# First phase of a two-layer hybrid decoder trunk: the state-space parameter work spread over sixteen steps, three modulation steps summed on VectorE

## The chip, the cores and the metric

The kernel runs on one core of one Trainium2 chip. The metric is the time of one execution on the device in microseconds (us), as the median of several runs. A second view is one profiled execution, whose trace lists each instruction of each engine with its start and its length. The engines are PE (TensorE, the matrix engine), DVE (VectorE), ACT (ScalarE), POOL (GpSimd) and SP (SyncE, which here only issues loads). Each engine takes its instructions in one fixed order; an instruction that waits holds all that stand behind it on its engine.

## The reference

The reference is a decoder trunk of two layers on 256 tokens of width 2048. What matters here is the head of layer 0:

```python
mod = jax.nn.silu(c) @ w_ada[layer] + b_ada[layer]
sh1, sc1, g1, sh2, sc2, g2 = jnp.split(mod, 6, axis=-1)
h = x * (1.0 + sc1[:, None, :]) + sh1[:, None, :]
...
proj = h @ w_in
...
dt = jnp.exp(log_dt)[:, None]
mag = jnp.exp(lam_re * dt)
lb_re = mag * jnp.cos(lam_im * dt)
lb_im = mag * jnp.sin(lam_im * dt)
...
_, _, x_re, x_im = lax.associative_scan(_complex_affine_combine, (a_re, a_im, bu_re, bu_im), axis=1)
```

A conditioning vector `c` gives a shift and a scale for each of the 2048 input channels (a matrix-vector product). The modulated input goes through the input projection `w_in`; one part of it, `u`, feeds a diagonal complex recurrence (S5) whose parameters (step size, decay, rotation, input and output matrices) are worked out from small weights that don't depend on the tokens. The other part feeds attention. Later come the output projection, layer norms, a SwiGLU block, and layer 1 with windowed attention. All is float32 in and out; a projection is made of three matrix products of split operands (a high part and a low part of each).

## The kernel before

**The first phase** is a loop over 16 steps `k`, one for each block of 128 input channels. All weights of the program come through a ring of 9 slots (`RING`), each a piece of 128x1024 float32 or less, in one fixed order on SP's queue; a piece is loaded when the piece nine places before it has been released. Each step takes six pieces. Four pieces (512 KB each, tensor `ada_s`) hold the columns of `w_ada` for the shift and the scale of the step's 128 channels; two pieces (384 KB each, `w_s`) hold 12 tiles of the input projection. A step does this:

- L660: 16 matmuls (the trace records each as two) multiply the four `ada_s` pieces with the conditioning vector into a PSUM bank `ab`; ACT copies the bank (L664), two small matmuls (L666) fold it to two columns, and DVE adds the bias (L668, tile `mod`): the step's shift and scale.
- DVE modulates the step's input (L670, tile `x`), ACT rounds it to the high part (L671, tile `hp`), and DVE subtracts for the low part (L672).
- `split` (L271 on ACT, L272 on DVE) makes the high part `wh` and the low part `wl` of each `w_s` piece, in three buffers (`NSPLIT`). The piece is released when both are done.
- 36 matmuls (L613, L614, L615) add the step to the banks of 12 output tiles. In this text they are the step's projection matmuls.

The bank `ab` is one, so the L660 matmuls of a step start only after the L668 of the step before.

**The recurrence's parameters** (`s5_params`, a generator) run beside the loop. Each call of `adv` takes the generator to its next `yield`; before, each step calls it twice (`EK[3]`). In the order of the code: step size and decay (128x32 operations, 12 to 20 in a chain), sine and cosine of the angle on ACT, four complex powers and three products as separate 128x32 operations (`cmul`, six operations each), then four quarters of a 128x2048 cosine and sine table (L470, L473, L474 on DVE, three activations L475 to L477 on ACT for each quarter), then the output matrices times the four powers (24 operations of 128x512, L485 to L491), then four quarters of the input matrices: six operations of 128x512 on DVE (L502 to L508), four activations on ACT (L511, tile `ebd`), 16 transposes on PE with four copies on ACT (L516, L517), 16 small matmuls `kc` (L524) and a copy on DVE (L528). Behind the loop the generator is run to its end. The table is first used after the phase, by the recurrence itself (L759, L760).

**What sets the order.** The code gives an order; a scheduler then reorders on each engine by its own estimate of the times, except that instructions marked with `front` are put ahead. So the place of the parameter work on an engine is neither that of the code nor fixed by hand. The loads keep the order of the code.

**After the loop** PE multiplies the forget-gate weights (L690), ACT copies the banks out (L703, L705) and re-lays `u` for the recurrence (L730), and the stream of weight pieces goes on: projection tiles (`w_ab`) and further pieces of `w_ada`. Most of those are multiplied and summed on DVE by one `tensor_tensor_reduce` for each piece (L544), with a row of the conditioning vector (`crow`), which steps 1 to 4 of the loop spread over the partitions.

Of the kernel before, what the change touches and what calls it, by code (L numbers as in the profile page):

```python
# [13 lines left out]
AF = mybir.ActivationFunctionType  # L14
# [16 lines left out]
FIRST = 3  # L31
EK = (1, 4, 1, 2)
HEAD = (10, 10, 10)
# [242 lines left out]
def build(tc, I, out):  # L276
# [3 lines left out]
    with ExitStack() as es:  # L280
# [98 lines left out]
        def s5_params():  # L379
# [5 lines left out]
            def tt(o, a, b, op):  # L385
                V.tensor_tensor(o, a, b, op)
# [22 lines left out]
            tt(th, lim, dt, ALU.mult)  # L409
            rho, sn, co, u0 = reg[8:12]  # L410
            V.tensor_scalar(t1, th, 1.0 / (2 * math.pi), MAGIC, op0=ALU.mult, op1=ALU.add)
# [12 lines left out]
            yield  # L424
            lr = [None, reg[12], reg[8], reg[10], reg[15]]
            li = [None, reg[13], reg[9], reg[14], reg[5]]
            tt(lr[1], mag, co, ALU.mult)
# [19 lines left out]

            def cmul(orr, oi, ar_, ai, br, bi):
                tt(t0, ar_, br, ALU.mult)
                tt(t1, ai, bi, ALU.mult)  # L450
                tt(t2, ar_, bi, ALU.mult)
                tt(t3, ai, br, ALU.mult)
                tt(orr, t0, t1, ALU.subtract)
                tt(oi, t2, t3, ALU.add)

            for k in (2, 3, 4):
                cmul(lr[k], li[k], lr[k - 1], li[k - 1], lr[1], li[1])
            for k in (1, 2, 3):
                cmul(wvr[:, 3 - k, :], wvi[:, 3 - k, :], lr[k], li[k], qr, qi)
            yield  # L460
# [6 lines left out]

            for qd in range(4):
                ca, sa = cosT[:, 512 * qd:512 * qd + 512], sinT[:, 512 * qd:512 * qd + 512]
                V.tensor_tensor(w1.rearrange("p (a j) -> p a j", j=64),  # L470
                                u0[:, 8 * qd:8 * qd + 8].rearrange("p (a o) -> p a o", o=1).to_broadcast([128, 8, 64]),
                                jrow.rearrange("p (o j) -> p o j", o=1).to_broadcast([128, 8, 64]), ALU.mult)
                V.tensor_scalar(w2, w1, MAGIC, -MAGIC, op0=ALU.add, op1=ALU.add)  # L473
                V.tensor_tensor(w1, w1, w2, ALU.subtract)  # L474
                A.activation(sa, w1, AF.Sin, scale=TWO_PI_LO)  # L475
                A.activation(ca, w1, AF.Abs)
                A.activation(ca, ca, AF.Sin, scale=-TWO_PI_LO, bias=hpi)  # L477
                yield

            V.tensor_scalar(gci[:, 0:512], gci[:, 0:512], -1.0, None, op0=ALU.mult)  # L480
            cr0, ci0 = a3(gcr[:, 0:512]), a3(gci[:, 0:512])
            for k in range(1, 5):
                orr = a3(g4[0]) if k == 4 else gcv[0][:, k]
                oi = a3(g4[1]) if k == 4 else gcv[1][:, k]
                V.tensor_tensor(orr, cr0, bc(lr[k]), ALU.mult)  # L485
                V.tensor_tensor(a3(w1), ci0, bc(li[k]), ALU.mult)
                V.tensor_tensor(orr, orr, a3(w1), ALU.add)
                yield
                V.tensor_tensor(oi, ci0, bc(lr[k]), ALU.mult)
                V.tensor_tensor(a3(w2), cr0, bc(li[k]), ALU.mult)  # L490
                V.tensor_tensor(oi, oi, a3(w2), ALU.subtract)  # L491
                yield

            eb = ebd.rearrange("p (c x g h) -> p c x g h", c=2, g=2, h=16)
            ebf = ebd.rearrange("p (c a m) -> p c a m", c=2, a=8)
            for qd in range(4):
# [30 lines left out]
                yield  # L527
                V.tensor_copy(kc[:, H], b[:, 0:128])  # L528


# [108 lines left out]
        ada0 = [scr[:, 256 * i:256 * i + 256] for i in range(2)]  # L639
        mod0 = c.small(32, "mod0")  # L640
        m0v = mod0.rearrange("p (t v) -> p t v", v=2)
        bad0 = c.small(32, "bad0")
# [11 lines left out]
        for k in range(KT):  # L654
            early.get(k, lambda: None)()
            for q in range(4):
                t = c.ptiles[6 * k + q]
                for j in range(4):
                    kk = 4 * q + j
                    PE.matmul(abank[32 * j:32 * j + 32, 0:256], lhsT=cs[:, kk:kk + 32], rhs=t[:, 256 * j:256 * j + 256],  # L660
                              start=(q == 0), stop=(q == 3), skip_group_check=True, tile_position=(0, 32 * j))
                c.release_piece(6 * k + q)
            a = ada0[k % 2]
            A.copy(a, abank[:, 0:256])  # L664
            for v in range(2):
                PE.matmul(abank[:, 256 + 2 * k + v:257 + 2 * k + v], lhsT=a[:, 128 * v:128 * v + 128],  # L666
                          rhs=sel4, start=False, stop=True, skip_group_check=True)
            V.tensor_tensor(m0v[:, k, :], abank[:, 256 + 2 * k:258 + 2 * k], b0v[:, k, :], ALU.add)  # L668
            xt = xs[k // 8][:, k % 8, :]
# [13 lines left out]
            if EK[2] <= k < EK[2] + 4:  # L683
                make_crow(k - EK[2])
            for _ in range(EK[3]):
                adv()
# [935 lines left out]
def _layout(x, c, positions, w_in_ab, b_forget, ssm_lambda_re, ssm_lambda_im, ssm_log_dt, ssm_b_re, ssm_b_im,  # L1622
# [8 lines left out]
    I = {}  # L1631
# [28 lines left out]
    s = a4[0][:, :, 0:2]  # L1660
    I["ada_s"] = np.ascontiguousarray(s.reshape(4, 4, 128, 2, 16, 128).transpose(4, 0, 2, 1, 3, 5)).reshape(64, 128, 1024)
    I["ada"] = _pack_ada(w_ada)

# [34 lines left out]
```

## Time and profile before

| | |
|---|---|
| median of 3 runs | 2275.93 us (2273.85 to 2277.19) |
| the profiled execution's own time | 2275.54 us |
| its span in the trace | 2273.8 us |
| PE busy | 2216.7 us (97% of the span) |
| DVE busy | 1719.1 us (76%) |
| ACT busy | 1131.8 us (50%) |
| bytes moved | 581.18 MB |

The span runs from the first to the last instruction in the trace; the execution's own time is 1.7 us longer. A busy time is the sum of an engine's instructions without overlap. Matmuls are pipelined, so a busy PE need not be one at its peak. The granted clock (PEclk) of a stretch is the share of the full matmul clock that the chip gave in it. DMA share is the mean busy share of the core's 16 DMA engines. In the rows, `a<-b` says which tile an instruction writes and which it reads, with buffer numbers left out; `x` behind a shape is a count; what stands in brackets is the idle time of the engine before the instruction and who ended it. In the chain of waits, the length of a matmul is the time until the next one starts.

### The profile page before, as it was taken

Reading aid. Unit: us, or ns where it says so; the run is one execution under the profiler, and the core shown is the slowest. Engines: PE = TensorE matmul, PEld = TensorE weight load, DVE = VectorE, ACT = ScalarE, POOL = GpSimd, SP = SyncE. Lnnn points to the kernel's source line nnn. Section 1 sums busy time; section 2 is a strip of 40 time slices with the busy share of each in tenths; the row PEclk is TensorE's granted clock in tenths of the full one; section 3 lists DMA queues with packets and bytes.
Section 4 is the critical chain, followed back from the end, with each engine's and each line's share of the span. In section 5 each row is a group of like instructions: output and inputs, shape, how many; then the busy total and the mean of one; then the engine's idle time right before and its main releaser. Section 6 shows DMA issues by size and latency. Waiting matters only on the chain.

```text
span 2273.8 us, 38500 instructions
## 1 busy us (share of the span) xinstructions
PE 2216.7 (97%) x14842; PEld 1940.3 (85%) x14842; DVE 1719.1 (76%) x3058; ACT 1131.8 (50%) x1820; POOL 2.3 (0%) x6
## 2 busy tenths in 40 slices
PE   6999999999999999999999999999999999999997
PEld 4778887889888888888888998899888888888886
DVE  7548887888888888888886999787776555555575
ACT  3456565365444334444444666575444334444444
POOL 0000000000000000000000000000000000000000
PEclk9999999999999999999999999999999999999998
DMA  9998787958999899999874876458887666666661
GB/s 342 356 330 326 277 304 257 340 169 293 321 318 321 319 320 315 319 320 320 317 243 152 288 230 215 132 160 273 266 269 244 186 186 187 190 187 188 189 186 68
DMA packets 161481, 581.18 MB, mean 256 GB/s; under 512 B 18320, under 2 KB 18960, under 8 KB 160912
## 3 DMA queue, kind: packets, MB, share of 16 engines
q1 hardware_dynamic: 159984, 575.49, 74.3%
q10 hardware_dynamic: 1312, 3.23, 0.4%
q8 instruction: 116, 1.90, 0.3%
q14 instruction: 69, 0.57, 0.1%
HBM read 576.55 MB, written 2.10 MB: 254 GB/s over the span
## 4 chain that ended last, share of the span: by engine, by line
PE 94%; DVE 3%; ACT 1%; DMA 1%; issue 0%; ACTq 0%; DVEq 0%
PE acc L618 43%; PE acc L619 22%; PE acc L613 6%; PE acc L614 6%; PE acc L615 6%; PE acc L1338 2%; PE aux L566 1%; PE ab L660 1%; DVE wl L272 1%; PE aux L1150 1%; PE aux L737 1%; PE aux L1183 0%; DMA w<-in_ada 0%; PE aux L815 0%; PE aux L1168 0%; ACT wh L271 0%
## 5 line engine op out<-in xcount | busy, mean ns | idle before, releaser
L618 PE MATMUL acc<-hp,wh 128*128 128x512 f32 x4212 | 1465.6, 397 | 3.6 <-DVE z L954 2.4
L272 DVE TENSOR_TENSOR wl<-w,wh 128x1024 fp32r<-128x1024 f32 (+1 forms) x712 | 862.2, 1212 | 402.4 <-ACT wh L271 387.1
L271 ACT CAST wh<-w 128x1024 fp32r<-128x1024 f32 (+1 forms) x712 | 740.2, 1040 | 847.6 <-PE acc L618 457.6
L619 PE MATMUL acc<-hp,wl 128*128 128x256 f32 x4212 | 1149.6, 280 | 0.5 <-DVE wl L272 0.5
L618 PEld LDWEIGHTS acc<-hp,wh 128*128 128x128 f32 x4212 | 778.3, 188 | 181.3 <-ACT lnb L974 2.7
L619 PEld LDWEIGHTS acc<-hp,wl 128*128 128x128 f32 x4212 | 795.1, 189 | 19.3 <-DVE wl L272 1.9
L544 DVE CUSTOM_DVE_ANT_0 w<-w,crow 128x1024 f32<-128x1024 f32 x280 | 340.7, 1218 | 0.0
L614 PE MATMUL acc<-hp,wh 128*128 128x256 f32 x1196 | 338.7, 290 | 1.5 <-DVE hp L672 0.8
L613 PE MATMUL acc<-hp,wh 128*128 128x256 f32 x1196 | 330.0, 290 | 10.2 <-ACT hp L671 5.1
L615 PE MATMUL acc<-hp,wl 128*128 128x256 f32 x1196 | 325.1, 289 | 0.0
L613 PEld LDWEIGHTS acc<-hp,wh 128*128 128x128 f32 x1196 | 225.9, 194 | 25.7 <-issue 7.6
L614 PEld LDWEIGHTS acc<-hp,wh 128*128 128x128 f32 x1196 | 232.3, 194 | 8.0 <-issue 4.6
L615 PEld LDWEIGHTS acc<-hp,wl 128*128 128x128 f32 x1196 | 224.8, 194 | 3.1 <-issue 2.9
L954 DVE SCALAR_TENSOR_TENSOR z<-acc,mod,z 128x256 f32<-128x256 f32 x176 | 83.7, 480 | 39.0 <-PE acc L619 27.8
L1260 ACT COPY ftmp<-acc 128x256 f32<-128x256 f32 x80 | 29.8, 372 | 117.2 <-PE acc L619 117.2
L1261 DVE TENSOR_TENSOR ftmp<-acc,ftmp 128x256 f32<-128x256 f32 x80 | 33.8, 422 | 28.2 <-ACT ftmp L1260 28.2
L660 PE MATMUL ab<-w,cs 128*32 128x256 f32 x512 | 35.2, 391 | 15.3 <-ACT cs L325 11.6
L1338 PE MATMUL acc<-wh,hp 128*128 128x512 f32 (+1 forms) x192 | 47.5, 357 | 0.0
L1338 PEld LDWEIGHTS acc<-wh,hp 128*128 128x128 f32 x192 | 33.9, 189 | 5.8 <-issue 0.8
L1265 DVE TENSOR_TENSOR ftmp<-ftmp 128x256 f32<-128x256 f32 x80 | 33.8, 423 | 4.7
L660 PEld LDWEIGHTS ab<-w,cs 128*32 128x32 f32 x512 | 15.4, 111 | 25.1 <-ACT cs L325 11.6
L1272 DVE TENSOR_TENSOR hp<-ftmp,hp 128x256 fp32r<-128x256 f32 x88 | 36.6, 420 | 0.1
(302 smaller groups left out, 1424.1 us busy)
## 6 DMA issues: line engine op xcount, KB each, us to landing
w<-in_w_gu SPq DMA_DIRECT2D x352, 512.0 KB, 4.4
w<-in_ada SPq DMA_DIRECT2D x320, 512.0 KB, 4.8
w<-in_w_dn SPq DMA_DIRECT2D x176, 512.0 KB, 4.3
w<-in_ada_s SPq DMA_DIRECT2D x64, 512.0 KB, 6.5
w<-in_w_ab SPq DMA_DIRECT2D x40, 512.0 KB, 5.8
w<-in_w_c SPq DMA_DIRECT2D x40, 512.0 KB, 4.1
w<-in_w_oab SPq DMA_DIRECT2D x32, 512.0 KB, 5.3
w<-in_w_oc SPq DMA_DIRECT2D x32, 512.0 KB, 3.8
```

Of the source, the lines that this page charges most:

```text
L271: self.front(nc.scalar.copy(wh[:, :n], src), "act")
L272: self.front(nc.vector.tensor_sub(wl[:, :n], src, wh[:, :n].bitcast(F32)))
L544: c.front(V.tensor_tensor_reduce(t, t, crow[:, 1024 * half:1024 * half + 1024], scale=1.0, scalar=0.0, op0=ALU.mult, op1=ALU.add, accum_ou ...
L613: PE.matmul(dst, lhsT=wh, rhs=hi_of(P, k), start=first, stop=False, skip_group_check=True)
L614: PE.matmul(dst, lhsT=wh, rhs=lo_of(P, k), start=False, stop=False, skip_group_check=True)
L615: PE.matmul(dst, lhsT=wl, rhs=hi_of(P, k), start=False, stop=last, skip_group_check=True)
L618: PE.matmul(bank, lhsT=wh, rhs=both_of(P, k), start=first, stop=False, skip_group_check=True)
L619: PE.matmul(bank[:, 256:512], lhsT=wl, rhs=hi_of(P, k), start=False, stop=last, skip_group_check=True)
L660: PE.matmul(abank[32 * j:32 * j + 32, 0:256], lhsT=cs[:, kk:kk + 32], rhs=t[:, 256 * j:256 * j + 256], start=(q == 0), stop=(q == 3), skip ...
L954: ins = V.scalar_tensor_tensor(zt(L, t), src, L["g"][:, t:t + 1], zt(L, t), op0=ALU.mult, op1=ALU.add)
L1272: V.tensor_sub(lo_of(F["ap"], f), a, hi.bitcast(F32))
L1338: PE.matmul(dst, lhsT=act[:, X], rhs=ww[:, c0:c0 + w], start=first, stop=(last and act is lo), skip_group_check=True)
```

## The change

The change does four things.

1. `adv` is called by a table: `PARTS[k]` times in step `k`, instead of twice.
2. The parameters' order is changed: the cosine and sine table is now the generator's last part, behind the four quarters of the input matrices; the fourth power of the output matrices comes after the first quarter.
3. `cmul` takes several powers in one operation: the powers lie side by side, and 36 operations of 128x32 become 18 of 128x32, 128x64 and 128x96. The products go to scratch in `et`.
4. In the steps 8, 11 and 14 (`ROWS`) the four `ada_s` pieces are not multiplied on PE. The host lays these pieces out transposed (same size, same order of loads), and DVE multiplies and sums each with half of `crow` (`tensor_tensor_reduce`, marked `front`) into one column of `rsum`; two small additions give the step's shift and scale. L660, L664 and L666 fall away in these steps.

```diff
-EK = (1, 4, 1, 2)
+EK = (1, 4, 1)
+ROWS = (8, 11, 14)
+PARTS = (2, 2, 1, 2, 2, 2, 2, 4, 0, 3, 3, 2, 3, 3, 0, 1)
...
-            def cmul(orr, oi, ar_, ai, br, bi):
-                tt(t0, ar_, br, ALU.mult)
-                tt(t1, ai, bi, ALU.mult)
-                tt(t2, ar_, bi, ALU.mult)
-                tt(t3, ai, br, ALU.mult)
-                tt(orr, t0, t1, ALU.subtract)
-                tt(oi, t2, t3, ALU.add)
-
-            for k in (2, 3, 4):
-                cmul(lr[k], li[k], lr[k - 1], li[k - 1], lr[1], li[1])
-            for k in (1, 2, 3):
-                cmul(wvr[:, 3 - k, :], wvi[:, 3 - k, :], lr[k], li[k], qr, qi)
+            def cmul(orr, oi, ar_, ai, br, bi, n):
+
+                p0, p1 = (x.rearrange("p (k a) -> p k a", a=32)[:, 0:n, :] for x in (et[:, 0:96], et[:, 128:224]))
+                br, bi = (x.rearrange("p (o a) -> p o a", o=1).to_broadcast([128, n, 32]) for x in (br, bi))
+                tt(p0, ar_, br, ALU.mult)
+                tt(p1, ai, bi, ALU.mult)
+                tt(orr, p0, p1, ALU.subtract)
...
+            cmul(pw_r[:, 2:3, :], pw_i[:, 2:3, :], pw_r[:, 3:4, :], pw_i[:, 3:4, :], lr[1], li[1], 1)
+            cmul(pw_r[:, 0:2, :], pw_i[:, 0:2, :], pw_r[:, 2:4, :], pw_i[:, 2:4, :], lr[2], li[2], 2)
+            cmul(wvr[:, 0:3, :], wvi[:, 0:3, :], pw_r[:, 1:4, :], pw_i[:, 1:4, :], qr, qi, 3)
...
-            for qd in range(4):
-                ca, sa = cosT[:, 512 * qd:512 * qd + 512], sinT[:, 512 * qd:512 * qd + 512]
...
-            for k in range(1, 5):
+
+            def out_power(k):
...
+            for k in range(1, 4):
+                yield from out_power(k)
...
                 V.tensor_copy(kc[:, H], b[:, 0:128])
+                if qd == 0:
+                    yield from out_power(4)
+
+            for qd in range(4):
+                ca, sa = cosT[:, 512 * qd:512 * qd + 512], sinT[:, 512 * qd:512 * qd + 512]
...
+                if k in ROWS:
+                    c.front(V.tensor_tensor_reduce(t, t, crow[:, 1024 * (q // 2):1024 * (q // 2) + 1024], scale=1.0, scalar=0.0,
+                                                   op0=ALU.mult, op1=ALU.add, accum_out=rsum[:, q:q + 1]))
+                else:
+                    for j in range(4):
...
+            if k in ROWS:
+                V.tensor_tensor(rsum[:, 0:2], rsum[:, 0:2], rsum[:, 2:4], ALU.add)
+                V.tensor_tensor(m0v[:, k, :], rsum[:, 0:2], b0v[:, k, :], ALU.add)
+            else:
...
-            for _ in range(EK[3]):
+            for _ in range(PARTS[k]):
                 adv()
```

**How the order of the instructions moves.** No time is in these rows. Lines of the changed kernel are a little higher: L272 is now L274, L668 is L689, L670 is L691, L660 is L677, L613 is L625, L690 is L711, and the new sums are L672.

DVE around step 7, before. `w_715` and `w_721` are the `w_s` pieces of step 6, `w_800` and `w_806` those of step 7, `w_885` is the first of step 8; the first `mod` is that of step 6, the second that of step 7.

```order
L272 TENSOR_TENSOR wl_846<-w_721,wh_845 128x768
L668 TENSOR_TENSOR mod_50_150<-ab_149,bad_51_151 128x2
L670 TENSOR_SCALAR x_76<-x_76,mod_50_150 128x256
L272 TENSOR_TENSOR wl_907<-w_800,wh_906 128x768
L672 TENSOR_TENSOR hp_122<-x_76,hp_122 128x256
L272 TENSOR_TENSOR wl_931<-w_806,wh_930 128x768
```

The next three rows on DVE before are `mod` and `x` of step 7 and a copy of `kc`. The same place in the changed kernel, where `w_768` and `w_774` are the `w_s` pieces of step 7, and `w_780`, `w_793`, `w_817` and `w_851` are the four `ada_s` pieces of step 8:

```order
L274 TENSOR_TENSOR wl_879<-w_768,wh_878 128x768
L505 TENSOR_TENSOR et_117<-ms_118,fl_82 128x512
L274 TENSOR_TENSOR wl_903<-w_774,wh_902 128x768
L672 ISA w_780,rsum_151<-w_780,crow_100 128x1024
L672 ISA rsum_151 128x1
L672 ISA w_793,rsum_151<-w_793,crow_100 128x1024
...
L689 TENSOR_TENSOR mod_50_150<-ab_149,bad_52_152 128x2
L672 ISA w_817,rsum_151<-w_817,crow_100 128x1024
...
L691 TENSOR_SCALAR x_76<-x_76,mod_50_150 128x256
L672 ISA w_851,rsum_151<-w_851,crow_100 128x1024
```

The `mod` and the `x` here are those of step 7. They now stand behind two and three sums over pieces of step 8, which come later in the stream of loads than all that step 7 needs; the low part of step 7 (L693) stands eight rows further on. At step 10 three sums of step 11 stand ahead of `mod` and all four ahead of `x`; at step 13 all four sums of step 14 stand ahead of `mod`. The four quarters of the table, last in the code, stand among the split, modulation and low-part rows of the steps 8 to 10.

PE at the end of the phase, before. `wh_1618` belongs to step 14, `wh_1706` to step 15; `w_1487` to `w_1567` are the `ada_s` pieces of step 15.

```order
L613 MATMUL kb_148<-hp_124,wh_1618 128x256
...
L660 MATMUL ab_149<-w_1487,cs_97 32x256 x4
...
L660 MATMUL ab_149<-w_1567,cs_97 32x256 x4
L516 MATMUL tr_1792<-cst_80,ebd_86 128x128 x4
L666 MATMUL ab_149<-cst_80,scr_120 128x1 x2
L516 MATMUL tr_1798<-cst_80,ebd_86 128x128 x4
L524 MATMUL kc_1804<-gcr_113,ebd_86 32x64
...
L690 MATMUL fb_1773<-x_77,wf_83 32x256 x8
L566 MATMUL aux_1857<-w_1691,cs_97 32x512 x2
L613 MATMUL acc_143<-hp_124,wh_1706 128x256
```

The changed kernel, where `wh_1498` belongs to step 13, `wh_1629` to step 14, `wh_1684` to step 15, and `w_1489` to `w_1589` are again the `ada_s` pieces of step 15:

```order
L677 MATMUL ab_149<-w_1489,cs_97 32x256 x4
...
L677 MATMUL ab_149<-w_1589,cs_97 32x256 x4
L625 MATMUL acc_143<-hp_124,wh_1498 128x256
...
L625 MATMUL kb_148<-hp_124,wh_1629 128x256
L687 MATMUL ab_149<-cst_80,scr_120 128x1 x2
L578 MATMUL aux_1798<-w_1669,cs_97 32x512 x2
L578 MATMUL aux_1798<-w_1675,cs_97 32x512 x2
L711 MATMUL fb_1738<-x_76,wf_83 32x256 x8
...
L625 MATMUL acc_143<-hp_124,wh_1684 128x256
```

The modulation matmuls of step 15 moved ahead of the projection matmuls of the steps 13 and 14, and no transposes and no `kc` are left between step 14 and step 15. The order of the loads on SP is the same in both kernels.

## Rows read from the trace of the kernel before

**Rows 1.** The page: busy time, share of the span and instructions of each engine.

```profile
PE 2216.7 (97%) x14842; PEld 1940.3 (85%) x14842; DVE 1719.1 (76%) x3058; ACT 1131.8 (50%) x1820; POOL 2.3 (0%) x6
```

**Rows 2.** Stretches: length, engines' busy us (instructions), granted clock, DMA share, GB/s.

```profile
core 0: us, PE busy (x) PEld busy (x) DVE busy (x) ACT busy (x) POOL busy (x), PEclk, DMA share, GB/s
28.00:72.00 44.00, 33.36 (x316) 26.50 (x320) 43.84 (x112) 21.05 (x38) 0.00 (x0) 0.96 0.91 344
72.00:161.00 89.00, 84.86 (x934) 69.95 (x923) 41.16 (x75) 41.51 (x75) 0.30 (x1) 1.00 0.92 335
40.00:45.00 5.00, 1.28 (x22) 0.62 (x15) 5.00 (x14) 1.74 (x4) 0.00 (x0) 1.00 0.69 219
45.00:50.00 5.00, 4.80 (x28) 4.50 (x28) 5.00 (x13) 3.04 (x6) 0.00 (x0) 0.66 1.00 399
```

**Rows 3.** Waits of PE, 160 to 600 us: total us, times, longest.

```profile
PE acc L613 <- ACT wh L271: 1.6, 1, 1.6
PE acc L613 <- ACT hp L1072: 1.1, 1, 1.1
```

**Rows 4.** Timeline of DVE: start us, length us, line, tiles.

```profile
33.52 0.95 DVE L386 TENSOR_TENSOR scr<-scr 128x32 f32<-128x32 f32 x8
...
38.89 0.15 DVE L668 TENSOR_TENSOR mod<-ab,bad 128x2 f32<-128x2 f32 x1
...
48.13 0.95 DVE L272 TENSOR_TENSOR wl<-w,wh 128x768 fp32r<-128x768 f32 x1
49.00 0.68 DVE L490 TENSOR_TENSOR et<-gcr,scr 128x512 f32<-128x512 f32 x1
49.60 0.68 DVE L486 TENSOR_TENSOR et<-gci,scr 128x512 f32<-128x512 f32 x1
...
57.15 0.42 DVE L672 TENSOR_TENSOR hp<-x,hp 128x256 fp32r<-128x256 f32 x1
57.48 0.69 DVE L491 TENSOR_TENSOR gci<-gci,et 128x512 f32<-128x512 f32 x1
...
71.90 0.41 DVE L670 TENSOR_SCALAR x<-x,mod 128x256 f32<-128x256 f32 x1
```

**Rows 5.** The chain of waits, steps 5 to 15: start us, us, what, matmuls.

```profile
73.32 0.67 PE acc L613 x4
...
120.08 0.12 PE acc L615
...
128.90 0.60 PE tr L516 x4
...
138.19 0.34 PE ab L666 x4
...
152.53 1.86 PE ab L660 x32
...
156.98 1.23 PE kc L524 x29
158.38 1.73 PE fb L690 x29
...
160.78 0.67 PE acc L613 x4
```

**Rows 6.** Timeline of DVE: sums over a piece, one behind the other.

```profile
152.07 1.22 DVE L544 CUSTOM_DVE_ANT_0 w<-w,crow 128x1024 f32<-128x1024 f32 x1
...
153.22 1.22 DVE L544 CUSTOM_DVE_ANT_0 w<-w,crow 128x1024 f32<-128x1024 f32 x1
```

**Rows 7.** Groups by line on ACT, 28 to 72 us: count, busy us, mean ns, idle.

```profile
L477 ACT ACTIVATE cos<-cos,hpe 128x512 f32<-128x512 f32 x4 | 2.9, 724 | 0.1
```

**Rows 8.** Timeline of ACT behind the phase.

```profile
167.90 9.45 ACT L730 COPY u<-u 32x256 f32<-32x256 f32 x14
177.37 1.04 ACT L271 CAST wh<-w 128x1024 fp32r<-128x1024 f32 x1
```

**Rows 9.** Timeline of PE: the projection matmuls of step 2 begin.

```profile
44.76 0.73 PE L613 MATMUL acc<-hp,wh 128*128 128x256 f32 x4 [3.72 <-ACT hp L671]
```

More of the change, by code (lines that the diff above doesn't have):

```diff
@@ L409, in s5_params @@
             tt(th, lim, dt, ALU.mult)
-            rho, sn, co, u0 = reg[8:12]
+            rho, sn, co = reg[8:11]
+            u0 = dt
             V.tensor_scalar(t1, th, 1.0 / (2 * math.pi), MAGIC, op0=ALU.mult, op1=ALU.add)
@@ L424, in s5_params @@
             yield
-            lr = [None, reg[12], reg[8], reg[10], reg[15]]
-            li = [None, reg[13], reg[9], reg[14], reg[5]]
+            pw_r, pw_i = (scr[:, 512 + 128 * i:640 + 128 * i].rearrange("p (k a) -> p k a", a=32) for i in (2, 3))
+            lr, li = ([None] + [x[:, 4 - k, :] for k in range(1, 5)] for x in (pw_r, pw_i))
             tt(lr[1], mag, co, ALU.mult)
@@ L640, in build @@
         mod0 = c.small(32, "mod0")
+        rsum = c.small(4, "rsum")
         m0v = mod0.rearrange("p (t v) -> p t v", v=2)
@@ L657, in build @@
                 t = c.ptiles[6 * k + q]
[L658 to L661, printed above, removed]
-                c.release_piece(6 * k + q)
[L663 to L668, printed above, removed]
+                if k in ROWS:
[3 more added lines that the diff above has]
+                    for j in range(4):
+                        kk = 4 * q + j
+                        PE.matmul(abank[32 * j:32 * j + 32, 0:256], lhsT=cs[:, kk:kk + 32], rhs=t[:, 256 * j:256 * j + 256],
+                                  start=(q == 0), stop=(q == 3), skip_group_check=True, tile_position=(0, 32 * j))
+                c.release_piece(6 * k + q)
+            if k in ROWS:
+                V.tensor_tensor(rsum[:, 0:2], rsum[:, 0:2], rsum[:, 2:4], ALU.add)
+                V.tensor_tensor(m0v[:, k, :], rsum[:, 0:2], b0v[:, k, :], ALU.add)
+            else:
+                a = ada0[k % 2]
+                A.copy(a, abank[:, 0:256])
+                for v in range(2):
+                    PE.matmul(abank[:, 256 + 2 * k + v:257 + 2 * k + v], lhsT=a[:, 128 * v:128 * v + 128],
+                              rhs=sel4, start=False, stop=True, skip_group_check=True)
+                V.tensor_tensor(m0v[:, k, :], abank[:, 256 + 2 * k:258 + 2 * k], b0v[:, k, :], ALU.add)
             xt = xs[k // 8][:, k % 8, :]
@@ L1661, in _layout @@
     I["ada_s"] = np.ascontiguousarray(s.reshape(4, 4, 128, 2, 16, 128).transpose(4, 0, 2, 1, 3, 5)).reshape(64, 128, 1024)
+    for k in ROWS:
+        rows = s[:, :, :, k].reshape(2, 1024, 2, 128).transpose(0, 2, 3, 1)
+        I["ada_s"][4 * k:4 * k + 4] = rows.reshape(4, 128, 1024)
     I["ada"] = _pack_ada(w_ada)
```

22 lines of the change are left out of this document (13 added, 9 removed).

## The prediction

> **What bounds the kernel now.** I read the page first. PE is busy for 97% of the span [rows 1]. For the first phase I therefore asked not which engine is busy but who keeps PE waiting, stretch by stretch. The stretches [rows 2] show two halves. From 28 to 72 us (steps 1 to 4) DVE is busy for 43.84 of 44 us and PE for only 33.36, at its worst for 1.28 of 5 us from 40 to 45: DVE sets the pace. From 72 to 161 us (steps 5 to 14, and what stands ahead of step 15's projection) PE is busy for 84.86 of 89 us and DVE for 41.16: PE sets the pace. In both halves the loads run at a DMA share of 0.91 and 0.92, so they leave 4.0 and 7.1 us, and no change of order can win more than these 11.1 us here. Behind the phase PE hardly waits: the longest wait between 160 and 600 us is 1.6 us [rows 3], and there PE runs its matmuls one behind the other. So what the first phase gains should reach the end of the kernel nearly whole, and what it loses too.
>
> **The sum is made of four terms**, against the profiled execution (2275.54 us, span 2273.8), which lies 0.4 us below the median of the runs. About 0.2%, 4.6 us, is what a measurement can tell from no change.
>
> *Start of step 5.* Prices on DVE, as start to start in a full queue [rows 4]: 0.60 us for 128x512, 0.87 for a split of 128x768, 0.33 for 128x256, 0.11 for 128x32. The widened complex products (128x64, 128x96) have no row; they lie between 0.11 and 0.33, nearer to the first by size, and since they stand with the small operations ahead of step 1's split, which waits for its load, I count them at nothing (at 0.33 each the twelve would cost 4 us less the eighteen operations saved, 2 us). From the `mod` of step 2 (38.89) to the `x` of step 5 (71.90) the order before has 38 operations of 512, 8 splits, 7 of 256, ten small ones and four `mod`s: 33.4 us by these prices, 33.0 in the trace. The changed order has 31, 8, 7 and no small ones: 28.2 us. Seven wide and ten small operations are gone from the stretch, table quarters above all. To the low part of step 4, however, it has 31 wide ones for 26, 25.7 us for 23.7, because input-matrix work moved forward: step 4 comes at 64.6, some 2 us later. From there PE leads: 36 projection matmuls at 0.12 us [rows 5] take 4.3 us, the folding 0.34, bias, modulation and rounding about 0.9, and three quarters of step 6's modulation matmuls (1.4) stand ahead: 71.5 instead of 73.3. **Minus 1.8 us**; bounds from plus 2 (step 4's delay stays) to minus 4.8 (DVE's count alone).
>
> *PE's work from there to step 15.* Modulation matmuls of three steps fall away: 3 x 1.86; their folding: 3 x 0.34 [rows 5]. One group of transposes (0.60) and ten of sixteen `kc` matmuls of the first quarter (1.3 for all sixteen by the 1.23 of 29 records, so 0.8) are done before step 5 now, in a stretch where PE has time. A quarter of step 6's modulation matmuls (0.5) comes later. The forget-gate matmuls (1.73) stay. Sum: **minus 7.5 us**, all on the engine that sets the pace.
>
> *New waits.* Twelve sums go to DVE, 1.15 us each, start to start [rows 6]: 13.8 us, and the table's twelve operations, 6.2 us, move into steps 8 to 10. DVE has 48 us free in this stretch, so its total isn't the matter; its order is. At the steps 7, 10 and 13 two to four sums over pieces of the next step stand ahead of `mod` or `x`. Behind them on DVE wait the low part and the splits, on ACT the high part, and PE's projection matmuls of the same step wait for all of it. Three sums, 3.45 us, less what PE has of its own there (folding 0.34, `kc` 1.3, a group of transposes 0.6) leave 1.2 us, three times: **plus 3.6 us**. Bounds: nothing, when DVE gets to the sums while the projection of the step before still runs, and 13.8 us, all twelve exposed. The table's twelve activations on ACT are at most 0.72 us each [rows 7], 8.7 us, among splits of the steps 8 to 10; I cost them at nothing because the projection matmuls of steps 7 and 8 now run one behind the other for 8.6 us. If that cover is gone, each split behind a table quarter is late by up to 2 us; that is inside the bound above.
>
> *Behind the phase.* Sixteen copies that re-lay `u` stand on ACT [rows 8]: 14 take 9.45 us, and the split at 177.37 behind them is PE's 1.6 us wait [rows 3]. In the new order eleven stand ahead of one more split and five ahead of this one, the same sixteen; but the first of these splits is later by eleven copies, 7.4 us, with two pieces' matmuls (5.8 us) to cover it. **Plus 0.7 us**, between 0 and 1.6.
>
> Total: -1.8 - 7.5 + 3.6 + 0.7 = -5.0 us, so 2270.5 us.
>
> The step of the sum with the largest bounds is the wait of PE, and there the matmul clock matters too. Before step 2's projection PE waited 3.72 us for ACT's high part [rows 9], and in the stretch that follows, 45 to 50 us, the granted clock is 0.66, a mean of 1.2 and 2.4 GHz, with 28 matmuls; the stretch is longer by a third of its 5 us, 1.7 us, than it would be at 2.4 GHz [rows 2]. My sum leaves the clock at 2.4 GHz, as the whole stretch from 72 to 161 us shows it. The Trainium skill (TensorE: Matmul & The Clock Gate, Part 1: The HAM clock gate) speaks against it: "the default state is throttled, and activity releases the throttle", so work taken off PE and put behind a wait can be paid for twice. By that rule a drop behind each new wait would make the sum -5.0 + 5.1, no gain; the trace agrees that the clock falls behind a wait, and shows no drop in the second half.
>
> **Rivals.**
>
> *The gain is eaten (chance 0.34).* The sums cover nothing: at each of the three places all four sums, 4.6 us, are exposed but for `kc` and transposes (1.9): 8.1 us in place of 3.6. For it: a load of the next step is by order the last thing to come, and the ring's nine places hold one and a half steps. Against it: the pieces summed come back to the ring sooner than PE returned them. Total -1.8 - 7.5 + 8.1 + 0.7 = -0.5: 2275.0 us.
>
> *Slower by the clock (chance 0.12).* The same waits, and behind each of the three the granted clock falls as in [rows 2, 9]: three times 1.7 us on top of the case above, 2280.1 us. It decides where PE stands idle behind the sums so that the stretch after it shows a granted clock below 1. Against it: PE's waits before were mostly short and the clock stayed full from 72 us on. The rule of the Trainium skill quoted above would have it so.
>
> *Slower by the waits alone (chance 0.05).* All twelve sums exposed: -1.8 - 7.5 + 13.8 + 0.7 = +5.2, 2280.7 us. It decides when every sum also waits for its load.
>
> *No new wait at all (chance 0.10).* -1.8 - 7.5 = -9.3: 2266.2 us. For it: PE's projection of the step before lasts 4.3 us, longer than three sums. Against it: the order puts them directly ahead of `mod`.
>
> That the change doesn't do what it says is no rival of weight: the table is "last" only in the code, and stands among steps 8 to 10 in the order; that is priced above.
>
> **How the numbers follow.** The forecast has a chance of 0.39; with the case without waits, faster by over 0.2% has 0.48. Within 0.2%: 0.35 (the eaten gain, and a little of the forecast's edge). Slower: 0.17. The forecast's own range is 2267 to 2274. The range over all cases goes from 2265.0, where the loads' 11.1 us of free time end it (2264.4), to 2280.0, which takes in the clock rival nearly whole and leaves out the worst waits.
>
> **What would show it.** Right: step 5's `x` before 70.5 us; PE's stretch from step 5 to step 15 some 5 to 6 us shorter; idle time of PE ahead of the projections of steps 7, 10 and 13, ended by ACT's high part behind a DVE sum, 2 us or less each; step 15's projection begins near 156 us instead of 160.78; the PE waits behind 160 us as before. Wrong: a granted clock under 1 between 80 and 150 us; idle time of 3 us or more at the three steps; the phase shorter but the end not, which would mean that something later waited for the loads.

## The result: slower by 0.7%, outside the range

The changed kernel takes 2293.25 us (median of 4 runs, 2291.12 to 2297.29), the kernel before 2275.24 us beside it (4 runs): a ratio of 1.0071, with a 95% interval of 1.006 to 1.0083 (the two medians by themselves give 1.0079). The forecast was 2270.5 us, the range 2265.0 to 2280.0. The profiled executions have spans of 2295.5 and 2273.8 us, so 21.7 us have to be found. The profiled execution of the changed kernel is the slowest of its four, 4.0 us above their median; that of the kernel before lies at its median.

The page of the changed kernel, busy time by engine (before: [rows 1]). PE has 13 us more to do by this count, though matmuls of three steps are gone:

```profile
PE 2229.5 (97%) x14734; PEld 1947.8 (85%) x14734; DVE 1731.2 (75%) x3067; ACT 1131.6 (49%) x1817; POOL 2.3 (0%) x6
```

Stretches of the changed kernel, with the columns of [rows 2]:

```profile
72.00:161.00 89.00, 78.70 (x767) 64.99 (x766) 54.42 (x104) 43.30 (x74) 0.30 (x1) 0.88 0.90 318
90.00:95.00 5.00, 2.52 (x37) 1.83 (x37) 4.58 (x12) 2.83 (x6) 0.00 (x0) 0.94 0.92 305
95.00:100.00 5.00, 4.29 (x22) 3.25 (x23) 5.00 (x14) 2.95 (x7) 0.30 (x1) 0.50 0.55 194
120.00:125.00 5.00, 1.99 (x12) 0.94 (x12) 4.96 (x14) 3.49 (x6) 0.00 (x0) 0.67 1.03 414
145.00:150.00 5.00, 2.38 (x42) 2.20 (x41) 5.00 (x8) 0.83 (x1) 0.00 (x0) 0.90 1.00 357
150.00:155.00 5.00, 4.59 (x36) 2.40 (x37) 3.10 (x11) 1.19 (x3) 0.00 (x0) 0.50 1.00 346
180.00:185.00 5.00, 2.67 (x16) 2.47 (x15) 0.44 (x1) 4.88 (x8) 0.00 (x0) 0.81 0.01 3
185.00:190.00 5.00, 5.00 (x25) 5.00 (x25) 4.19 (x6) 4.93 (x8) 0.00 (x0) 0.50 0.60 197
```

From 72 to 161 us the mean granted clock is 0.88 where it was 1.00. At three places (steps 7, 10 and 13) PE stands for about half of 5 us, and DVE is busy there; right behind each the clock is at 0.50 to 0.67. The same happens once more behind the phase, from 180 us on. Step 10 in the changed kernel, timeline of DVE and PE (start us, length us; in brackets the idle time before and who ended it):

```profile
118.05 0.50 PE L687 MATMUL ab<-cst,scr 128*128 128x1 f32 x4
118.08 1.22 DVE L672 CUSTOM_DVE_ANT_0 w<-w,crow 128x1024 f32<-128x1024 f32 x1
...
119.61 0.28 PE L522 MATMUL kc<-gci,ebd 128*32 128x64 f32 x2
...
120.37 1.22 DVE L672 CUSTOM_DVE_ANT_0 w<-w,crow 128x1024 f32<-128x1024 f32 x1
...
121.51 0.15 DVE L689 TENSOR_TENSOR mod<-ab,bad 128x2 f32<-128x2 f32 x1
121.58 1.21 DVE L672 CUSTOM_DVE_ANT_0 w<-w,crow 128x1024 f32<-128x1024 f32 x1
...
122.72 0.28 DVE L526 COPY ms<-kc 128x128 f32<-128x128 f32 x1
...
122.93 0.40 DVE L691 TENSOR_SCALAR x<-x,mod 128x256 f32<-128x256 f32 x1
...
123.01 1.08 PE L677 MATMUL ab<-w,cs 128*32 128x256 f32 x8 [3.12 <-DVE ms L526]
```

PE had folded step 10's modulation by 118.55 (L687). `mod` runs at 121.51, behind three sums over pieces of step 11, and `x` at 122.93, behind the fourth and the copy of `kc`: some 4 us late. PE still has its `kc` matmuls, to 119.9; its next instructions are the modulation matmuls of a later step, which wait for DVE too. At step 7 a second queue adds to it: `x` runs at 92.30, and on ACT the four `ebd` activations stand ahead of the high part. PE's four waits there (0.68, 0.68, 1.36 and 0.75 us) all end with ACT; those at the steps 10 and 13 (3.12 and 3.03 us) end with DVE.

```profile
93.10 2.56 ACT L509 ACTIVATE ebd<-et,cst 128x512 f32<-128x512 f32 x4 [1.42 <-PE kc L522]
95.57 0.39 ACT L692 CAST hp<-x 128x256 fp32r<-128x256 f32 x1
```

Where the clock is halved, the length of the matmuls shows it: at 150.41 us the 32 modulation matmuls of a step take 3.64 us, against 1.86 in [rows 5].

```profile
150.41 3.64 PE L677 MATMUL ab<-w,cs 128*32 128x256 f32 x32 [3.03 <-DVE mod L689]
```

Behind the phase, waits of PE from 160 to 600 us (before: [rows 3], longest 1.6), and the rows at that wait:

```profile
PE aux L758 <- ACT kT L726: 2.3, 1, 2.3
```

```profile
174.53 5.27 ACT L751 COPY u<-u 32x256 f32<-32x256 f32 x8
...
180.44 1.93 ACT L751 COPY u<-u 32x256 f32<-32x256 f32 x3
182.39 1.07 ACT L726 COPY kT<-kb 128x512 f32<-128x512 f32 x2
183.03 5.30 PE L758 MATMUL aux<-u,el 128*128 128x64 f32 x24 [2.33 <-ACT kT L726]
```

Eleven of the sixteen re-laying copies stand ahead of what PE needs, and the 24 matmuls behind the wait run at half clock.

**Where the 21.7 us are.** Four markers cut the two traces: the start of step 5's projection, the first matmul of L1338 (L1359 in the changed kernel), and in the attention of the second layer the first rotation matmul (L1116, L1137) and the last product with v (L1183, L1204). The expectations below call the second marker the glu stage. Their rows before:

```profile
199.34 0.70 PE L1338 MATMUL acc<-wh,hp 128*128 128x512 f32 x2
...
1293.74 1.02 PE L1116 MATMUL aux<-qf,cst 128*128 128x256 f32 x4
...
1447.53 1.52 PE L1183 MATMUL aux<-pb,kvrot 128*64 128x256 f32 x16
```

And in the changed kernel:

```profile
214.49 0.70 PE L1359 MATMUL acc<-wh,hp 128*128 128x512 f32 x2
...
1308.52 1.02 PE L1137 MATMUL aux<-qf,cst 128*128 128x256 f32 x4
...
1469.28 1.52 PE L1204 MATMUL aux<-pb,kvrot 128*64 128x256 f32 x16
```

Step 5 starts 1.3 us later, from there to L1359 go 13.9 us more, and a further 7.0 us are lost 1.1 ms later, in an attention whose code and data the change doesn't touch. The rest (-0.5) is spread. So there were two things to explain, and the total alone would have hidden one of them.

### The profile page after: what moved, and what is told of

It is laid out like the page before. It is cut to its first block, busy times and chain, and to the rows that moved or that the text cites. A ratio compares the mean times of both kernels' runs of the same rounds, so it can differ in the third digit from the quotient of the medians.

```text
span 2295.5 us, 38289 instructions
## 1 busy us (share of the span) xinstructions
PE 2229.5 (97%) x14734; PEld 1947.8 (85%) x14734; DVE 1731.2 (75%) x3067; ACT 1131.6 (49%) x1817; POOL 2.3 (0%) x6
## 4 chain that ended last, share of the span: by engine, by line
PE 93%; DVE 3%; ACT 2%; DMA 1%; issue 1%; ACTq 0%; DVEq 0%
PE acc L630 43%; PE acc L631 21%; PE acc L625 6%; PE acc L626 6%; PE acc L627 6%; PE acc L1359 2%; PE ab L677 1%; DVE wl L274 1%; PE aux L758 1%; PE aux L578 1%; PE aux L1171 1%; PE aux L1204 1%; ACT wh L273 1%; DMA w<-in_ada 0%; PE aux L1189 0%
## 5 line engine op out<-in xcount | busy, mean ns | idle before, releaser
L274 DVE TENSOR_TENSOR wl<-w,wh 128x1024 fp32r<-128x1024 f32 (+1 forms) x712 | 862.4, 1212 | 420.2 <-ACT wh L273 408.1
L625 PE MATMUL acc<-hp,wh 128*128 128x256 f32 x1196 | 332.3, 293 | 6.2 <-ACT hp L1093 3.4
L625 PEld LDWEIGHTS acc<-hp,wh 128*128 128x128 f32 x1196 | 228.4, 197 | 19.0 <-issue 6.6
L677 PE MATMUL ab<-w,cs 128*32 128x256 f32 x416 | 35.0, 463 | 19.8 <-ACT cs L327 11.2
L1359 PE MATMUL acc<-wh,hp 128*128 128x512 f32 (+1 forms) x192 | 47.2, 356 | 0.0
L1359 PEld LDWEIGHTS acc<-wh,hp 128*128 128x128 f32 x192 | 34.0, 189 | 5.9 <-issue 0.8
L677 PEld LDWEIGHTS ab<-w,cs 128*32 128x32 f32 x416 | 12.3, 124 | 30.3 <-ACT cs L327 11.2
```

The source lines that it names most:

```text
L274: self.front(nc.vector.tensor_sub(wl[:, :n], src, wh[:, :n].bitcast(F32)))
L625: PE.matmul(dst, lhsT=wh, rhs=hi_of(P, k), start=first, stop=False, skip_group_check=True)
L1359: PE.matmul(dst, lhsT=act[:, X], rhs=ww[:, c0:c0 + w], start=first, stop=(last and act is lo), skip_group_check=True)
```

## The experiments

All times from the profiled execution of each kernel, in us; the ratio is of the runs' times to the kernel before.

| kernel | step 5 starts | from there to L1338/L1359 | second layer's attention | ratio (95%) |
|---|---|---|---|---|
| before | 73.2 | 126.1 | 155.3 | |
| changed | 74.5 | 140.0 | 162.3 | 1.0071 (1.006 to 1.0083) |
| no sums | 73.9 | 128.8 | 160.1 | 1.0031 (1.0019 to 1.0043) |
| sums only | 74.6 | 130.7 | 162.2 | 1.0091 (1.0077 to 1.0104) |
| sums behind | 74.6 | 134.6 | 155.4 | 1.0016 (1.0005 to 1.0027) |
| filler | 74.3 | 140.0 | 155.1 | 1.0078 (1.0066 to 1.0091) |
| short sums | 74.2 | 124.5 | 163.1 | 1.0036 (1.0023 to 1.0049) |
| one step | 74.4 | 128.8 | 160.1 | 1.0033 (1.0021 to 1.0045) |
| two steps | 74.7 | 134.9 | 160.0 | 1.0056 (1.0041 to 1.0071) |
| short filler | 72.7 | 136.5 | 162.7 | 1.0054 (1.0037 to 1.0071) |
| late order | 74.9 | 140.0 | 155.4 | 1.0028 (1.0018 to 1.0038) |
| before, late order | 76.5 | 125.9 | 160.0 | 1.0022 (1.0011 to 1.0033) |
| sums after low part | 74.1 | 127.1 | 155.1 | 0.9999 (0.9989 to 1.0008) |
| before, sums after low part | 73.3 | 126.3 | 162.7 | 1.0045 (1.0031 to 1.0058) |

The second column of times can be trusted to some tenths, as far as two pairs show it: the kernels with the same order of the first phase (changed and late order, before and before with late order) agree within 0.2. The first column can't: the second of these pairs has 73.2 and 76.5.

**No sums.** The three steps go back to PE; the parameter work stays as changed.

```diff
-ROWS = (8, 11, 14)
+ROWS = ()
```

> The changed kernel, but all sixteen steps keep their modulation on PE (no step on VectorE; the parameter work stays spread, its tables last, its products batched). If the sums on VectorE cost the time (they stand ahead of the modulation and x of steps 7, 10 and 13, PE idles and its clock drops): no granted clock below 0.95 between 72 and 161 us, step 15's projection about 1 to 3 us earlier than the 160.8 of the kernel before, time 2270 to 2276 us. If the spread parameter work costs it: still 2288 to 2294 us, and the dips near 95, 120 and 150 us stay. If each costs half: about 2283 us.

The clock is back, and so is most of the time in the phase, but not in the total:

```profile
72.00:161.00 89.00, 85.34 (x928) 67.76 (x920) 44.89 (x82) 45.50 (x80) 0.30 (x1) 1.00 0.95 336
```

128.8 us against 140.0: beside the spread parameter work the sums cost 11.2 us. Against 126.1 that parameter work costs 2.7 by itself; step 15's projection starts at 162.6 us, not earlier than before. The expected time (2270 to 2276 us) was missed too, at 2285.3, mainly by the second layer: 160.1 us in an attention whose code is that of before.

**Sums only.** The reverse: parameter work as before, sums as changed.

```diff
+ROWS = (8, 11, 14)
...
+                if k in ROWS:
+                    c.front(V.tensor_tensor_reduce(t, t, crow[:, 1024 * (q // 2):1024 * (q // 2) + 1024], scale=1.0, scalar=0.0,
```

> The kernel before with the modulation of steps 8, 11 and 14 summed on VectorE and nothing else of the change. If the sums cost the time: 2288 us or more, at best a little under the changed kernel's 2293, granted clock below 0.95 between 72 and 161 us with dips behind steps 7, 10 and 13. If the parameter work costs it: 2268 to 2276 us, the saved matmuls are gained or the time is as before. If both are needed (table quarters of steps 8 to 10 beside the sums): 2276 to 2284 us.

The total fits the first theory, and PE waits for `mod` at the three steps, but the stretches say otherwise: in the first phase the sums cost 4.6 us here (130.7 against 126.1), and from there to the second layer's attention 10 us more go (1104.4 us, 1094.4 before), again in stages that the edit doesn't touch.

```profile
PE ab L666 <- DVE mod L678: 9.3, 3, 3.3
```

So sums alone (4.6) and parameter work alone (2.7) make 7.3 of the changed kernel's 13.9 us. The other 6.6 come only where both are changed; what in their meeting costs them, no run separates. Totals alone couldn't be read any more; the column by stretches is used from here on.

**Sums behind.** `mod`, `x` and the low part of steps 7, 10 and 13 get the same mark as splits and sums, which orders them as the code has them.

```diff
+            if k + 1 in ROWS:
+                c.front(xi)
```

(likewise for `mod` and the low part)

> The changed kernel with the modulation, x and low part of steps 7, 10 and 13 held ahead of the sums of the next step on VectorE; the same sums, the same matmuls. If the loss is the order (sums ahead of what PE waits for): PE's idle time at these steps shrinks below 2 us each, the granted clock stays above 0.95 from 72 to 161 us, time 2266 to 2276 us. If PE, with the matmuls of three steps taken off it, has too little to do at the pace of the loads whatever the order: dips of the granted clock remain, 2282 to 2292 us.

Half a hit: 134.6, so 5.4 of the 11.2 us come back, but by the ranges set beforehand it falls in the other case (granted clock 0.93 from 72 to 161 us, 2282.6 us). The order now holds the splits of a step behind its low part, and the loads pause because their nine slots are full:

```profile
90.00:95.00 5.00, 4.52 (x54) 4.30 (x54) 4.26 (x7) 2.05 (x4) 0.00 (x0) 1.00 0.37 110
115.00:120.00 5.00, 3.81 (x59) 3.13 (x58) 2.49 (x6) 3.29 (x7) 0.00 (x0) 1.00 0.45 153
```

**Filler and short filler.** Useless matmuls on PE ahead of the three projections, to hold the clock up while it waits.

```diff
+            if k + 1 in ROWS:
+                for i in range(NFILL):
+                    j = i % 4
+                    c.front(PE.matmul(abank[32 * j:32 * j + 32, 288:512], lhsT=cs[:, 0:32], rhs=crow[:, 0:224], ...), "pe")
```

> The changed kernel with 48 useless matmuls (32x224, four at a time on quarters of the array, about 2.5 us a group) ahead of the projections of steps 7, 10 and 13, where PE waits for the sums; the sums stay ahead of the modulation there. If most of the loss is the clock that drops behind the wait: the dips near 95, 120 and 150 us become smaller and the time falls by 5 to 11 us, to 2282 to 2288 us, although work was added. If the loss is the waits themselves: 2293 to 2301 us, no gain, or the 7.5 us of added matmuls on top. Each wait's end (the high part of the step) should stand where it was relative to its loads in both cases.

> As the run with the filler, but 20 useless matmuls a group (about 1 us at full clock) instead of 48, so that they end before the high part is there. If the clock that drops behind the wait costs the time: dips smaller than in the changed kernel and the glu stage 2 to 6 us earlier than its 214.5 us. If the place of the sums alone costs it: 213 to 216 us whatever the clock shows; the same if so short a filler doesn't keep the clock up.

With 48 a group the clock is nearly full, and the phase is as long as without:

```profile
72.00:161.00 89.00, 82.01 (x1004) 67.11 (x1003) 53.29 (x102) 42.46 (x72) 0.31 (x1) 0.98 0.83 303
```

With 20 a group it is 3.5 us shorter. By the ranges set beforehand the long filler speaks for the waits (2296.8 us) and the short one for the clock (the glu stage at 209.1 us). Neither settles what the clock is worth: the long filler ends after the high part is there (step 7's comes at 92.52 us, its projection at 95.8), and both moved other rows of the order: at step 7 ACT now makes the high part ahead of the four `ebd` activations. That part is left open.

**Short sums.** Each sum takes 64 columns of 1024.

```diff
-c.front(V.tensor_tensor_reduce(t, t, crow[:, 1024 * (q // 2):1024 * (q // 2) + 1024], scale=1.0, scalar=0.0,
+c.front(V.tensor_tensor_reduce(t[:, 0:64], t[:, 0:64], crow[:, 0:64], scale=1.0, scalar=0.0,
```

> The changed kernel, but each of the twelve sums takes 64 of the 1024 columns of its piece; the rest of those products is left out. PE's saved matmuls stay saved, VectorE's 13.8 us of sums fall to some 2 us. If VectorE's time in the sums is the cost: the first matmul of the glu stage (214.5 us in the changed kernel, 202.7 without sums, 199.3 before) comes at 195 to 201 us, the granted clock from 72 to 161 us is above 0.97. If the loads set the pace once PE has less to do: 201 to 204 us, as without sums, with PE idle behind loads and the DMA share above 0.93. If PE with less work drops its clock whatever the sums take: above 206 us.

124.5 us: where the sums stand ahead, DVE's time in them is what costs. It is also the most that taking these matmuls off PE brought in any run: 4.3 us less than with no sums, 1.6 less than before, with sums that cost next to nothing. Other waits are left in it: the granted clock is 0.67 from 120 to 125 us.

**One step and two steps.**

```diff
-ROWS = (8, 11, 14)
+ROWS = (8,)
```

(and `(8, 11)`)

> The changed kernel with one step (8) summed on VectorE instead of three. If each place costs by itself: the first matmul of the glu stage 3 to 5 us behind the 202.7 us of the kernel without sums, one dip of the granted clock near 95 us and none near 120 and 150; time about 2288 us. If only the third place or the end of the phase costs: within 1 us of 202.7.

> The changed kernel with two steps (8 and 11) summed on VectorE. If each place costs by itself: 6 to 9 us behind 202.7, two dips of the granted clock, time about 2292 us. If the loads give back what one place loses (their queue of nine pieces fills while PE waits): the same as with one step.

With one step there is the wait and the drop of the clock, as in the changed kernel: PE is busy for 2.52 of the 5 us from 90 on, and the granted clock is 0.50 in the next 5. Yet the phase is as long as with none: 128.8. Against the loss stand the 2.2 us of matmuls that one place saves. The second place brings 6.1 us, the third 5.1. The expectation that each costs by itself was wrong for the first; why it is free and the second is not, these runs don't tell apart.

**Late order, in the changed kernel and in the one before.** Four and five fills of a spare tile on DVE in the first layer's last stage make the scheduler lay out the second layer anew, and nothing in the first phase.

```diff
+            if ph == "d01":
+                for _ in range(4):
+                    c.front(V.memset(nudge, 0.0))
```

> The changed kernel with four fills of a spare 128x512 tile on VectorE where the first layer's last stage begins, far behind the first phase. The first phase keeps the changed kernel's order row by row; the attention of the second layer comes out of the scheduler in the order of the kernel before, row by row. If the last 7 us of the changed kernel's loss are that order: the glu stage still begins near 214.5 us, the second layer's attention (first rotation matmul to last product with v) takes 155 us instead of 162, time 2284 to 2288 us. If they follow from the first phase (later loads, another state of the buffers): 162 us again, 2291 to 2295 us.

> The kernel before with five such fills at the same place: the first phase keeps its order, and the second layer's attention comes out in the order, row by row, of the changed kernel without sums, where it took 160 us instead of 155. If that order is what those 5 us are: 160 us there, and 2280 to 2283 us for a kernel whose first phase is untouched. If the time there follows from the first phase: 155 us, 2275 to 2278 us (five fills are 2 to 3 us of an engine that has time).

Both came out as the first of the two cases had it. The changed kernel with before's order on PE in that attention:

```profile
214.94 0.70 PE L1359 MATMUL acc<-wh,hp 128*128 128x512 f32 x2
...
1308.94 1.02 PE L1137 MATMUL aux<-qf,cst 128*128 128x256 f32 x4
...
1462.78 1.52 PE L1204 MATMUL aux<-pb,kvrot 128*64 128x256 f32 x16
```

The first phase is as slow as ever, the attention takes 155.4 us again, and the ratio falls from 1.0071 to 1.0028. The kernel before, with the order that the kernel without sums has there, takes 160.0 us and 0.2% more in total, with no edit to the first phase. The other runs agree: three kernels with before's order of PE's rows in that attention (before, sums behind, late order) take 155.3 to 155.4 us there, and four that share another one (no sums, one step, two steps, before with late order) 160.0 or 160.1. The 7 us go with the order there, not with the first phase.

**Sums after the low part.** One dependency: the first sum of a step waits for the low part of the step before. The splits stay free to run ahead.

```diff
+                    if q == 0:
+                        c.also_after(ti, low)
```

> The changed kernel with one dependency added: the first sum of the steps 8, 11 and 14 waits for the low part of the step before, so the sums stand behind the modulation, x and low part of steps 7, 10 and 13, and the splits of these steps stay ahead of them. If the place of the sums is what PE waits for: no idle time of 2 us or more at the three steps, granted clock above 0.97 from 72 to 161 us, the glu stage at 198 to 204 us (214.5 in the changed kernel, 202.7 without sums). If the loads' nine places, held by pieces that wait for their sums, make up for it: 206 to 212 us with pauses in the loads, as when all of mod, x and low part were held ahead of the splits too.

> The kernel before with the sums of steps 8, 11 and 14, each group behind the low part of the step before; parameter work as before. If the place of the sums was the loss and the spread parameters cost 3 us by themselves: the glu stage at 195 to 200 us, at or ahead of the 199.3 of before. If sums cost wherever they stand: 203 us or later.

Timeline of DVE at step 7 with the changed kernel's parameter work: `mod`, `x` and low part first, the four sums behind them.

```profile
88.89 0.16 DVE L692 TENSOR_TENSOR mod<-ab,bad 128x2 f32<-128x2 f32 x1 [0.39 <-PE ab L690]
89.08 0.41 DVE L694 TENSOR_SCALAR x<-x,mod 128x256 f32<-128x256 f32 x1
90.30 0.43 DVE L696 TENSOR_TENSOR hp<-x,hp 128x256 fp32r<-128x256 f32 x1 [0.81 <-ACT hp L695]
90.76 1.22 DVE L672 CUSTOM_DVE_ANT_0 w<-w,crow 128x1024 f32<-128x1024 f32 x1
```

127.1 us: 12.9 of the changed kernel's 13.9 us in this stretch are gone with the same sums, the same matmuls and one dependency more, though other rows move with it. PE's modulation matmuls wait for `mod` for 0.3 us in all, in the changed kernel for 3.4. The scheduler also happens on a quick order for the second layer, and the kernel is level with the one before (0.9999, interval 0.9989 to 1.0008). One pause is left, at step 10, so that the clock over 72 to 161 us is 0.96 and not above 0.97 as expected. The loads pause there, because pieces that wait for their sums hold the slots; PE's own idle time there ends with ACT. `x` is ready at 117.94 us, but the high part runs at 119.54, behind `ebd` and three activations of the table, which the forecast had put at nothing:

```profile
118.04 0.90 PE L514 MATMUL tr<-cst,ebd 128*128 128x128 f32 x3 [0.90 <-ACT ebd L509]
...
119.54 0.39 ACT L695 CAST hp<-x 128x256 fp32r<-128x256 f32 x1
```

```profile
115.00:120.00 5.00, 2.28 (x22) 1.51 (x18) 2.40 (x7) 4.82 (x10) 0.00 (x0) 0.79 0.60 220
120.00:125.00 5.00, 5.00 (x24) 5.00 (x25) 4.96 (x8) 1.77 (x3) 0.00 (x0) 0.52 0.44 123
```

With the parameter work of before, the first phase takes 126.3 us, as before (the expectation had it 0 to 4 us quicker), and the second layer falls to a slow order (162.7). Its runs went from 2282.3, the profiled one, to 2291.9; what the others lost beyond the order isn't known. None of the twelve is faster than the kernel before by more than a measurement can tell.

## Why the prediction was wrong

The step that failed most is the term *New waits*: its 3.6 us left out that the clock would fall behind the waits, and counted on cover that wasn't enough; 12.5 us were lost there. Two steps beside it failed: the term *Behind the phase* (0.7 us for 5.3), and the step from the first phase to the end of the kernel, which had no term for a new order of later stages (7.0 us).

**Start of step 5, forecast -1.8, measured +1.3.** The count of DVE's operations was right: step 4's low part was put at 64.6 us and came at 64.88. What failed is "from there PE leads" at full clock with little ahead: 6.9 us by the forecast to step 5's projection, 9.6 in the trace. PE is idle for 1.87 of the 5 us from 60 on, the clock falls to 0.87 and then 0.79, and step 4's projection starts at 66.9 against 62.8. Step 5's `x` runs at 72.15 (71.90 in [rows 4]); "before 70.5" was the test, and it failed.

```profile
60.00:65.00 5.00, 3.13 (x33) 1.42 (x32) 5.00 (x12) 1.88 (x4) 0.00 (x0) 0.87 0.96 364
65.00:70.00 5.00, 5.00 (x37) 3.86 (x38) 1.26 (x2) 1.85 (x4) 0.00 (x0) 0.79 0.97 341
```

The clock is only a part of it. The run with late order has the same order and a clock of 1.00 in both slices; its low part of step 4 runs at 66.80, and step 5's projection starts at 74.9, 8.1 us later. Between the two projections stand a group of transposes (71.78 to 72.34) and, directly ahead of step 5's, ten `kc` matmuls (twenty records, 73.66 to 74.49), which the next term of the forecast counted as done "in a stretch where PE has time". And the start itself differs by more than 3 us between two executions of one order (73.2 and 76.5 in the table), so that +1.3 and -1.8 are hardly told apart.

```profile
64.88 0.42 DVE L693 TENSOR_TENSOR hp<-x,hp 128x256 fp32r<-128x256 f32 x1
...
73.66 0.27 PE L522 MATMUL kc<-gcr,ebd 128*32 128x64 f32 x2
```

**PE's work, forecast -7.5.** The matmuls are gone, but work taken off the engine that is "busy for 84.86 of 89 us" isn't all time won: with sums of nearly no cost 4.3 us of the 6.6 arrive, and in the last run, with the sums behind the low part, none (126.3 us for 126.1): PE then waits for others, 4.8 us for ACT's `ebd` (2.0 before) and 1.9 for loads. The rest of the term, transposes and `kc` done earlier, didn't arrive at all: without sums the stretch is 2.7 us longer, with the loads at 0.95. What makes it longer isn't shown.

**New waits, forecast +3.6, bounds 0 to 13.8.** This term failed. The stretch from step 5's projection to the end of step 15's, in the changed kernel and in the one without sums:

```profile
74.50:174.90 100.40, 88.01 (x826) 72.12 (x824) 60.29 (x113) 49.94 (x89) 0.30 (x1) 0.90 0.90 321
```

```profile
73.90:168.40 94.50, 88.81 (x928) 71.00 (x930) 47.54 (x86) 50.43 (x92) 0.30 (x1) 1.00 0.94 335
```

PE is idle for 12.4 us against 5.7: 6.7 us of waits. Its busy time is only 0.8 us less although 3 x 2.2 = 6.6 us of work fell away. The other 5.8 us go with the half clock, but for the matmuls of two later pieces, 1.1 us, which stand inside this stretch here and just behind it without sums. Together 12.5 us, near the upper bound of 13.8, which the forecast had read as "all twelve sums exposed" and given to a rival with a chance of 0.05. The mechanism (sums ahead of `mod` and `x`, steps 7, 10 and 13, two to four sums at a time) was right; the cover counted against it was there in part. At step 10 the folding and the `kc` matmuls do run beside the sums (118.05 to 119.9); the transposes and the modulation matmuls that follow themselves wait for DVE or ACT ([3.12 <-DVE ms L526] above).

**"My sum leaves the clock at 2.4 GHz".** It falls at all three places, as the rival "slower by the clock" had it and as the test "a granted clock under 1 between 80 and 150 us" was to show. That rival, at 2280.1 us, was right in kind, and for this stretch nearly in size: 8.1 us of waits and 5.1 of clock, 13.2 against the 12.5 measured. It fell 17 us short by the other terms, ahead of and behind this stretch. The rule of the Trainium skill that the prediction quoted (TensorE: Matmul & The Clock Gate, Part 1: The HAM clock gate: "activity releases the throttle") agrees with these rows: 0.50 behind the waits at 90 and 145 us, 1.00 throughout without them. What full clock would have given back in the same order isn't shown by any run here.

**Behind the phase, forecast +0.7, at most 1.6.** From the end of step 15's projection to L1359 go 39.6 us (214.5 less 174.9), 34.3 without sums and 34.0 before: +5.3 to +5.6. The eleven copies ahead were foreseen, and the wait grew by only 0.7 us (2.3 for 1.6). What was not priced is the drop of the clock behind it: PE's busy time is 4.6 us longer than without sums, with two pieces' matmuls fewer.

```profile
174.90:214.49 39.59, 37.26 (x265) 35.18 (x264) 24.66 (x37) 30.26 (x43) 0.00 (x0) 0.87 0.66 226
```

```profile
168.40:202.70 34.30, 32.70 (x272) 30.55 (x273) 24.20 (x39) 30.20 (x43) 0.00 (x0) 1.00 0.73 261
```

**What had no term: "what the first phase gains should reach the end of the kernel nearly whole, and what it loses too".** The order of the later stages was taken as given. It comes from the same scheduler, and changed with edits to the first phase alone; it cost 7.0 us in the second layer's attention.

So: +1.3, +13.9 (12.5 of waits and clock, 2.7 of parameter work, 5.3 behind the phase, less 6.6 of matmuls) and +7.0, less 0.5 elsewhere.

## What to carry to other kernels

Work that moves to an engine with time to spare must be placed in that engine's order: look at what stands behind it there and who waits for that, and if it isn't needed at once, tie it behind the hand-over with a dependency. Idle time of a busy matrix engine is paid twice where its clock falls behind the wait, as in these runs, so a bound of "all of it exposed" isn't a remote case. Where a scheduler lays out the program, an edit can change stages that it doesn't touch: compare stretch by stretch between markers, and before a verdict check whether the order of the untouched stages is still the same.

## What was not expected of the hardware

The same instructions of the second layer's attention, with the same data, took from 155.1 to 163.1 us by their order. Part of it is what the first phase shows, a wait and a lower clock behind it. In the changed kernel PE waits 2.1 us there, 1.8 of them once for `pb`, and the granted clock is 0.71 in the 5 us behind. With the quick orders PE has no wait there and a clock of 1.00. In each kernel that takes 160 us or more PE stands idle for 2.1 to 4.0 us and has the lower clock.

```profile
PE aux L1189 <- ACT pb L1192: 1.8, 1, 1.8
```

```profile
1445.00:1450.00 5.00, 3.17 (x24) 2.22 (x25) 3.63 (x13) 4.89 (x16) 0.00 (x0) 0.95 0.07 13
1450.00:1455.00 5.00, 5.00 (x36) 3.83 (x33) 2.12 (x5) 1.47 (x4) 0.00 (x0) 0.71 0.29 98
```

By these rows the wait and the clock (0.05 and 0.29 of 5 us, 1.7) make some 3.8 of the 7 us, an estimate; in the rest PE is busy for longer, and why is open.

Two executions with the same order up to step 15 started step 5 at 73.2 and 76.5 us; the loads of the later one moved 317 GB/s from 28 to 72 us instead of 344. Such a spread is larger than the gain that was forecast for that stretch, and only the stretch behind it, 126.1 and 125.9 us, could be compared.
